# A two-layer mLSTM and pooling block: input sums stored in HBM and read back behind the last value tile, and a 128-byte filler

## The chip, the cores and the metric

The kernel runs on one core of a Trainium2 chip. The metric is the device time of one execution in microseconds (us). The engines are named as the profile names them: PE is TensorE (PEld its weight loads), DVE is VectorE, ACT is ScalarE, POOL is GpSimd and SP issues the DMAs.

## The reference

The model has two layers on 1024 latent tokens (model width 1024, inner width 2048) with 256 context tokens. Layer 0 is a bidirectional mLSTM mixer. Its input `h`, the normed and modulated tokens, is multiplied by three weight blocks:

```
xm, z, og = split(h @ w_in, 3)          # each 2048 wide
xc = silu(short_conv(xm)); q, k = headwise(xc); v = headwise(xm)
gates = [q, k, v] @ w_gate              # input and forget gates, both directions
y = (sigmoid(og) * norm(mlstm(q, k, v, gates)) + skip * xc) * silu(z);  out = y @ w_out
```

Layer 1 is a pooling mixer on the 16 x 64 token grid. The change touches layer 0 only: the forming of operands for the `z` and `og` products, and one address.

## The kernel before, in words

Every product is made from three fp32r matmuls: an fp32 operand `x` is split into a rounded part `hi` and a rest `lo`, and `hi*hi + hi*lo + lo*hi` is summed in PSUM (`mm3`, lines 142 to 145). So the layer's input lies in SBUF as pairs of tiles, `h[k, hf]` for the eight blocks k of 128 channels and the two halves hf of 512 tokens.

The work is staged as follows.

1. **Features** (lines 339 to 376, loop 491 to 500). For n = 0 to 15, PE forms 128 columns of `xm` for all tokens, and ACT and DVE form the convolution. The loop lies in a hand-written PE order. Between its matmuls stand those of `token_part(n - 1)` (lines 378 to 410): ten small products give the values of the previous tile, and DVE reduces each of them into a tile `vst` (line 397). The value tile of n = 15, the last, is left over, and is done between the first ten steps of the next stage.
2. **Block sums** (lines 503 to 519). For k = 0 to 3, POOL adds hi and lo of `h[k]` and `h[k+4]` back to fp32 into two tiles `t0`, `t1` (line 508). DVE forms four differences and sums of their halves (lines 512 to 515), ACT rounds each (518), and DVE takes the rest (519). The result is `T_[1..4, k]`, the right-hand operands of four products of a Strassen scheme.
3. **Plain products** (`plain`, lines 591 to 607). The first pair of `z` tiles and the first pair of `og` tiles are formed without Strassen. `count` numbers their 64 steps, each of three matmuls of 512 columns. Steps 1 to 10 pull the last value tile along. At steps 12, 15, 27 and 50 (`GATE_STEPS`) a piece of `gates()` (lines 416 to 487) follows: copies of the gate sums; transposes (423) and a chain of small DVE operations (424 to 450); transposes (457) and the running scans (466 to 470) with what follows them (474 to 477); and the last transposes (482, 486).
4. **Strassen products** (`strassen`, lines 526 to 567) for the 14 remaining pairs: seven products of four blocks in place of eight. In order they are a11 with plain `h`, s2 with `T_[2]`, s3 with `T_[3]`, a12 with plain `h`, s1 with `T_[1]`, a22 with `T_[4]`, and s4 with plain `h`. POOL forms s1 to s4 from the weights (lines 535 to 538).
5. **Scores and values** of 4 heads x 8 token tiles (lines 703 to 797, about 675 to 1270 us). In `values` (773), 30 matmuls per step have as weights the decayed scores, transposed into the tiles `pt` (`turn`, 757 to 766), and move value tiles `S4`.
6. The output product of layer 0, layer 1, and the output.

**Buffers.** Tiles are drawn by tag. The tag `T5` has five buffers in this part (the profile writes `T`), and the features' tiles `xp`, `y` and `vst`, the sums' `t0` and `t1`, the gates' tiles (`g32`, `lft`, `it_`, `lf_r`, `i_r`, `b_r`, `m_r`) and the Strassen tiles `r2`, `s12` and `s34` all draw from it. A tile waits until an earlier tile of its tag has had its last use. `S4` (profile: `S`) has 32 buffers of 4096 bytes, `wh`, `wl` and `wr` two of 4096 each, `pt` six of 2048. One pool holds them in the order in which they are first named: `S4`, `wh`, `wr`, `wl`, then `cst` (1152 bytes), `mask` (512), `amat` (256), then `pt`, then `hn` (three of 2048) and smaller tiles; the `T5` pool lies behind.

**Order.** Except for the hand-written stretches of PE, a scheduler that simulates the engines' times sets the order of each engine's instructions when the program is built. On the chip each engine takes its instructions in that order, and SP issues the DMAs in that order too.

## Time and profile before

| | us |
|---|---|
| median of 3 runs (2099.69 to 2103.97) | 2099.81 |
| the profiled execution, its own time | 2102.29 |
| its span, first to last instruction | 2100.6 |

PE is busy for 95% of the span, DVE for 64%, ACT for 37% and POOL for 23%. Busy time of PE includes matmuls that run at half clock, so a busy PE is not always a fast one. All times of day below are us from the start of the span.

### The profile page before, as it was taken

To read this page: it belongs to the slowest core of one execution; us is meant where nothing else is said; L and a number is where in the kernel's file an instruction comes from. 1 tells how busy PE (TensorE), PEld (TensorE's weight loads), DVE (VectorE), ACT (ScalarE), POOL (GpSimd) and SP (SyncE) were. 2 spreads that over 40 slices of the span, in tenths; PEclk is the share of its full clock that TensorE was granted. 3 is DMA by queue.
4 is the path that set the end of the run, shared out by engine and by line. 5 is a ranking of instruction groups with operands and counts; after the bars stand their busy time and mean duration, and the time that the engine had idled before them with its cause. 6 is when DMAs were issued, how large, how long until landed. Compare 5 with 4: busy or idle time off the path is not lost.

```text
span 2100.6 us, 26372 instructions
## 1 busy us (share of the span) xinstructions
PE 1994.7 (95%) x10050; PEld 1673.2 (80%) x10050; DVE 1335.8 (64%) x2136; ACT 773.3 (37%) x1201; POOL 486.5 (23%) x482
## 2 busy tenths in 40 slices
PE   7899996799999899999999999999999999999997
PEld 5688885688888787787878787888788888888897
DVE  4877777976777868667676663353567273754444
ACT  5444443333333533433324332443433132223443
POOL 4400003233222313331332311161200000000275
PEclk9999998899999999999999999999999999999999
DMA  7133332154443635245234143434331222124473
GB/s 295 73 113 108 104 107 88 49 163 146 141 131 121 230 126 154 77 147 164 81 110 151 41 157 129 171 131 140 120 121 56 78 73 71 60 96 158 157 263 126
DMA packets 156032, 263.94 MB, mean 126 GB/s; under 512 B 10077, under 2 KB 89437, under 8 KB 155905
## 3 DMA queue, kind: packets, MB, share of 16 engines
q1 hardware_dynamic: 155904, 262.25, 37.5%
q8 instruction: 79, 1.29, 0.2%
q14 instruction: 49, 0.39, 0.1%
HBM read 201.21 MB, written 61.00 MB: 125 GB/s over the span
## 4 chain that ended last, share of the span: by engine, by line
PE 66%; DVE 9%; POOL 3%; DMA 3%; issue 3%; ACT 1%; SPq 0%; DVEq 0%; POOLq 0%; ACTq 0%
PE pa L131 30%; PE pc L131 29%; PE pb L131 5%; PE pb L762 1%; DMA wr<-in_w_ada_dram 1%; POOL hn L931 1%; POOL S L951 1%; DVE wl L631 1%; DVE T L753 1%; DVE T L721 1%; DVE T L755 1%; DVE den L749 1%; PE pc L793 1%; DVE T L754 0%; DVE S L863 0%
## 5 line engine op out<-in xcount | busy, mean ns | idle before, releaser
L131 PE MATMUL pa<-S,wh 128*128 128x512 f32 (+1 forms) x2496 | 721.4, 373 | 8.3 <-DVE S L303 8.2
L131 PEld LDWEIGHTS pa<-S,wh 128*128 128x128 f32 x2496 | 444.7, 190 | 80.9 <-DVE S L303 11.9
L131 PE MATMUL pa<-S,wl 128*128 128x512 f32 (+1 forms) x1248 | 460.1, 369 | 0.4 <-DVE wl L139 0.3
L131 PE MATMUL pc<-S,wh 128*128 128x512 f32 (+1 forms) x1616 | 452.6, 366 | 2.8 <-ACT wh L137 1.9
L131 PEld LDWEIGHTS pc<-S,wh 128*128 128x128 f32 x1616 | 293.0, 189 | 53.0 <-ACT wh L137 2.1
L139 DVE TENSOR_TENSOR wl<-wr,wh 128x1024 fp32r<-128x1024 f32 (+1 forms) x124 | 146.8, 1184 | 272.3 <-ACT wh L137 271.3
L131 PE MATMUL pc<-S,wl 128*128 128x512 f32 (+1 forms) x808 | 294.1, 366 | 1.2 <-DVE wl L139 1.0
L137 ACT ACTIVATE wh<-wr 128x1024 fp32r<-128x1024 f32 (+1 forms) x124 | 124.6, 1005 | 404.8 <-PE pa L131 177.7
L131 PEld LDWEIGHTS pa<-S,wl 128*128 128x128 f32 x1248 | 236.0, 189 | 40.8 <-DVE wl L139 1.0
L131 PE MATMUL pa<-S,S 128*128 128x512 f32 (+1 forms) x1152 | 253.1, 369 | 14.5 <-DVE T L721 14.5
L131 PE MATMUL pc<-S,pt 128*128 128x512 f32 x960 | 237.6, 401 | 0.0
L131 PEld LDWEIGHTS pa<-S,S 128*128 128x128 f32 x1152 | 196.3, 194 | 46.8 <-issue 11.5
L131 PEld LDWEIGHTS pc<-S,pt 128*128 128x128 f32 x960 | 180.1, 191 | 39.5
L131 PEld LDWEIGHTS pc<-S,wl 128*128 128x128 f32 x808 | 152.6, 189 | 26.4 <-DVE wl L139 1.8
L931 POOL TENSOR_TENSOR hn<-hn,pt 128x512 f32<-128x512 f32 (+1 forms) x48 | 80.6, 1681 | 298.6 <-ACT pt L930 288.2
L764 ACT ACTIVATE pt<-pb 128x512 fp32r<-128x512 f32 (+1 forms) x96 | 48.7, 522 | 180.8 <-PE pb L762 138.6
L397 DVE TENSOR_REDUCE T<-pb 128x144 f32<-128x288 f32 x160 | 72.3, 454 | 59.6 <-PE pb L131 59.3
L721 DVE SCALAR_TENSOR_TENSOR T<-pa,T 128x256 f32<-128x256 f32 (+3 forms) x184 | 76.6, 454 | 36.9 <-PE pa L131 31.1
L642 POOL TENSOR_TENSOR S<-S,S 128x1024 fp32r<-128x1024 f32 x35 | 89.2, 2567 | 41.7 <-ACT S L641 41.7
L765 DVE TENSOR_TENSOR pt<-pb,pt 128x512 fp32r<-128x512 f32 (+1 forms) x96 | 56.5, 597 | 37.2 <-ACT pt L764 36.7
L545 ACT ACTIVATE wh<-T 128x512 fp32r<-128x512 f32 x70 | 42.5, 626 | 99.2 <-POOL T L538 55.6
L131 PE MATMUL pb<-S,wh 128*128 128x512 f32 x256 | 78.9, 389 | 0.0
(322 smaller groups left out, 2529.6 us busy)
## 6 DMA issues: line engine op xcount, KB each, us to landing
wr<-in_bw_in_dram SPq DMA_DIRECT2D x40, 512.0 KB, 3.5
wr<-in_w_in_dram SPq DMA_DIRECT2D x34, 512.0 KB, 3.8
S<-xc_d SPq DMA_DIRECT2D x34, 512.0 KB, 5.2
wr<-in_w_ada_dram SPq DMA_DIRECT2D x32, 512.0 KB, 3.7
wr<-in_w_out_dram SPq DMA_DIRECT2D x32, 512.0 KB, 3.5
T<-in_bw_out_dram SPq DMA_DIRECT2D x32, 512.0 KB, 4.4
S<-y_d SPq DMA_DIRECT2D x28, 512.0 KB, 7.0
v_d<-T SPq DMA_DIRECT2D x16, 640.0 KB, 3.9
```

The costliest lines, as they stand in the source:

```text
L131: PE.matmul(out, lhsT, rhs, start=start, stop=stop)
L137: S.activation(h, r, AF.Copy)
L139: V.tensor_tensor(l, r, f(h), op=ALU.subtract)
L397: V.tensor_reduce(vst[:, s], p.rearrange("p a b -> p b a"), axis=AX.X, op=ALU.add)
L545: S.activation(hi, a, AF.Copy)
L631: V.scalar_tensor_tensor(a, w, csil[:, k, 0:1], a, op0=ALU.mult, op1=ALU.add)
L642: eng.tensor_tensor(t, f(t), f(u), op=ALU.subtract)
L721: V.scalar_tensor_tensor(W[:, lo + sh:hi + sh], p[:, lo - o:hi - o], 1.0, W[:, lo + sh:hi + sh], op0=ALU.mult, op1=ALU.mult, accum_out=dp[ ...
L749: V.tensor_tensor(r, r, emt[:, ti, h:h + 33:32], op=ALU.max)
L764: S.activation(th[:, :n], p[:, :n], AF.Copy)
L765: V.tensor_tensor(tl_[:, :n], p[:, :n], f(th[:, :n]), op=ALU.subtract)
L931: G.tensor_tensor(acc, acc, sq, op=ALU.add)
```

## The change

Each of POOL's additions is done earlier, one k per feature tile n = 2 to 9, into an `S4` tile, and the fp32 sum is stored in HBM (`h_d`). The block sums become a function `sums(k)` that is called at steps 16, 24, 32 and 40 of the plain products. It loads `t0` and `t1` from `h_d` in place of having POOL add them; the DVE and ACT operations are the same as before. A tile `pad1` of 128 bytes per partition, which nothing uses, is named between `amat` and the first `pt` tile.

```diff
+SUM_STEPS = (16, 24, 32, 40)
...
+    h_d = dr.tile([KD, P, T], F32, name="h_d")
...
     amat = const([P, KE, 4], "amat")
+    const([P, 32], "pad1")
...
             if n == 2:
                 bilinear()
+            if 2 <= n < 2 + KD:
+                hs = tl("S4", [P, T])
+                for hf in range(2):
+                    G.tensor_tensor(hs[:, hf * 512:hf * 512 + 512], f(h[n - 2, hf][0]), f(h[n - 2, hf][1]), op=ALU.add)
+                nc.sync.dma_start(h_d[n - 2], hs)
             parts.append(token_part(n, *out))
...
         T_ = {}
-        for k in range(4):
+
+        def sums(k):
             t0, t1 = tl("T5", [P, T]), tl("T5", [P, T])
             for t, kk in ((t0, k), (t1, k + 4)):
-                for hf in range(2):
-                    G.tensor_tensor(t[:, hf * 512:hf * 512 + 512], f(h[kk, hf][0]), f(h[kk, hf][1]), op=ALU.add)
+                nc.sync.dma_start(t, h_d[kk])
             b11, b12, b21, b22 = t0[:, :512], t0[:, 512:], t1[:, :512], t1[:, 512:]
...
                         if count in GATE_STEPS:
                             next(steps, None)
+                        if count in SUM_STEPS:
+                            sums(SUM_STEPS.index(count))
```

## Rows read from the trace of the kernel before

**Rows 1.** The page, its head and busy times.

```profile
span 2100.6 us, 26372 instructions
PE 1994.7 (95%) x10050; PEld 1673.2 (80%) x10050; DVE 1335.8 (64%) x2136; ACT 773.3 (37%) x1201; POOL 486.5 (23%) x482
```

**Rows 2.** What PE waited for: in total, times, longest.

```profile
PE pb L131 <- DVE T L397: 27.7, 1, 27.7
```

**Rows 3.** Busy time by stretch; the clock is after POOL's count.

```profile
core 0: us, PE busy (x) PEld busy (x) DVE busy (x) ACT busy (x) POOL busy (x), PEclk, DMA share, GB/s
330.00:346.00 16.00, 16.00 (x92) 13.79 (x92) 10.71 (x19) 6.08 (x9) 5.09 (x4) 1.00 0.29 94
...
349.70:377.50 27.80, 0.07 (x1) 0.00 (x0) 27.49 (x25) 7.51 (x12) 20.34 (x12) 0.56 0.09 37
377.50:383.00 5.50, 5.50 (x16) 4.37 (x17) 5.50 (x11) 3.19 (x5) 0.63 (x1) 0.50 0.01 1
383.00:391.20 8.20, 8.20 (x42) 6.40 (x41) 7.83 (x17) 2.90 (x5) 0.14 (x1) 0.97 0.18 53
391.20:434.70 43.50, 41.36 (x207) 33.41 (x207) 34.15 (x47) 14.30 (x23) 12.75 (x7) 1.00 0.34 107
```

**Rows 4.** DVE in order of time around the stall: start, duration, line, operands.

```profile
352.21 1.76 DVE L512 TENSOR_TENSOR T<-T,T 128x512 f32<-128x512 f32 x1
...
371.26 0.68 DVE L512 TENSOR_TENSOR T<-T,T 128x512 f32<-128x512 f32 x1
...
375.33 1.75 DVE L514 TENSOR_TENSOR T<-T,T 128x512 f32<-128x512 f32 x1
377.00 0.81 DVE L397 TENSOR_REDUCE T<-pb 128x144 f32<-128x288 f32 x2
...
379.91 1.88 DVE L519 TENSOR_TENSOR S<-T,S 128x512 fp32r<-128x512 f32 x3
```

**Rows 5.** POOL in order of time; in brackets its idle time and what ended it.

```profile
334.35 2.55 POOL L508 TENSOR_TENSOR T<-S,S 128x512 f32<-128x512 f32 x2 [17.38 <-DVE T L365]
...
373.22 3.31 POOL L508 TENSOR_TENSOR T<-S,S 128x512 f32<-128x512 f32 x2 [3.04 <-DVE S L519]
...
414.99 2.60 POOL L535 TENSOR_TENSOR T<-T 128x512 f32<-128x512 f32 x1 [23.30 <-DVE T L470]
417.66 2.16 POOL L536 TENSOR_TENSOR T<-T,wr 128x512 f32<-128x512 f32 x1
```

**Rows 6.** PE in order of time, gate transposes and the second Strassen product.

```profile
391.19 0.80 PE L423 MATMUL pb<-ident,T 32*128 32x32 f32 x10
...
401.95 0.40 PE L457 MATMUL pb<-ident,T 128*36 128x128 f32 x2 [0.38 <-ACT T L458]
...
434.52 0.62 PE L131 MATMUL pc<-S,wh 128*128 128x512 f32 x2
```

**Rows 7.** DVE in order of time, scans and what follows them.

```profile
402.80 0.68 DVE L466 TENSOR_TENSOR_SCAN hn<-T,zero 36x256 f32<-36x256 f32 x1 [2.40 <-ACT T L458]
403.51 2.34 DVE L467 TENSOR_TENSOR_SCAN T<-T,hn,zero 36x1024 f32<-36x1024 f32 x1
...
412.51 2.34 DVE L470 TENSOR_TENSOR_SCAN T<-T,hn,T 4x1024 f32<-4x1024 f32 x1
...
418.70 2.20 DVE L477 TENSOR_TENSOR T<-T,T 36x1024 f32<-36x1024 f32 x1
420.83 0.73 DVE L577 SCALAR_TENSOR_TENSOR hn<-hn,vec,pt 128x512 f32<-128x512 f32 x1
```

**Rows 8.** DMA issues from 340 to 440 us: KB each, median us to landing.

```profile
v_d<-T SPq DMA_DIRECT2D x2, 640.0 KB, 4.1
T<-in_w_in_dram SPq DMA_DIRECT2D x2, 512.0 KB, 3.7
```

**Rows 9.** Line 508, POOL's additions: duration in ns, minimum, median and maximum.

```profile
L508 POOL TENSOR_TENSOR T<-S,S x16: 1287/1674/2513, 334.3 to 374.8; 128x512 f32<-128x512 f32 x16
```

**Rows 10.** The chain that ended last: start, duration, matmuls of one run.

```profile
434.68 2.72 PE pc L131 x12
...
761.80 6.97 PE pc L131 x30
...
782.13 2.73 PE pa L131 x12
```

## The prediction

> **What bounds the kernel now.** I read the page first: PE is busy for 1994.7 of 2100.6 us [rows 1], so only the 106 us in which PE idles, stretches at half clock, and the matmuls' own pace can be won. The view of PE's waits comes next; its longest single wait is 27.7 us, on one DVE reduction of a value tile [rows 2]. The table of stretches places it: PE does nothing from 349.7 to 377.5, DVE is full (27.49 of 27.80) and POOL nearly so. [...]

> The timeline of DVE says why. From 352.2 DVE forms block sums; the first reduction for the last value tile (line 397) starts at 377.00, just after the work on the second k [rows 4]. In the code the four pairs `t0`, `t1` are named before the last `vst`, and they share five T5 buffers. The reader is to see that the reduction has no buffer until a block sum gives one back. POOL bears out that buffers go in the order of naming: it could add at any time, but began at 334.35, when line 365 of the feature tile gave a buffer up, and later additions begin when line 519 has [rows 5].

> **The change, part by part.** The sum is made against the profiled execution, 2102.29 us; it stands 2.5 above the median of 2099.81, and I carry the difference over to that median.

> *The stall goes.* The last `vst` is now named before any `t0`, so PE walks on at 349.7. Up to the gate transposes (line 423, at 391.19 [rows 6]) it has 5.5 us of work at half clock, 2.75 at full, and 8.2 us at nearly full [rows 3], together 11.0. These transposes come at 360.7; I take 361.0, since ten reductions and the convolution keep DVE nearly full there. So far 30 us are won: 27.7 of idle, 2.75 of clock.

> *How much is kept depends on the second Strassen product* (s2 with `T_[2]`), which starts at 434.52 [rows 6] and needs line 519's results of all four k. PE could be there at 404.0 (434.5 - 27.7 - 2.75). In the new order of naming the T5 buffers go: `vst`, `g32`, `lft`, `it_`, `lf_r`, `i_r`, two pairs of `t`, `b_r`, `m_r`, two more pairs, `r2`, `s12`, `s34`. Five buffers make this a ring, which I follow step by step.
> - The last 457 transposes of `lft` end at 402.35 [rows 6], 11.2 us after line 423; now at 372.2. Only then has the second tile of pair 0 a buffer. A load of the same size lands after 3.7 us [rows 8]: 375.9.
> - One k is four sums and four rests on DVE. Three rests took 1.88 us [rows 4], so 0.63 each and 5.0 per k, undisturbed. Pair 0 is free at 380.9, its first tile near 380.3.
> - That buffer goes to pair 1 (load to 384.0), the other to `b_r`. Now scans of `b` run as well: two of 0.68 and two of 2.34 [rows 7], 6.0. Pair 1's 5.0, these 6.0 and, as an estimate, 3.4 of gating work and weight rests end at 395.3. Pair 1, earlier in the program, is through near 390.5 and gives `m_r` and one tile of pair 2 their buffers.
> - The scans of `m` (6.0) and one gating step (1.5, two of 0.73 [rows 7]) end at 402.5. `lf_r` is free, and pair 2 can be loaded: 406.2.
> - Lines 474 to 477, the store of `i_r` (bounded by 4.1, the larger store of [rows 8]) and the transposes of `b_r` free two buffers by 407: pair 3 is there at 410.7, `r2` at about 410.
> - Pair 2 is through at 411.2. In pair 3 the needed rest lies 3.1 us further, 414.3. But POOL forms s1 and s2 then, and beside POOL a DVE sum took 1.76 in place of 0.68 [rows 4], POOL's own steps 2.60 and 2.16 [rows 5]. That moves both operands to about 417.

> So s2 starts near 417 in place of 434.5: 17.5 us. PE runs out of other work before: it could start s2 at 404, and a12, ahead of its turn, takes 2.72 [rows 10], to 407. Ten idle us follow, and they cost the clock once more, some 2.7 as before, and the product done early gives 2.7 back. For work of DVE that is still behind (two gating steps) I add 1. Stage: -16.5. The bounds are -30.5 (PE never waits) and, with every DVE step beside POOL, a loss (rival 2).

> *Sixteen additions and eight stores move to feature tiles 2 to 9, eight loads to the plain products.* POOL idled 17.38 us there before its first addition [rows 5], so 2 x 1.67 us per tile [rows 9] fit. DVE steps beside them lengthen by some 1.1 each, and PE waits on DVE's reductions. But in 330 to 346 POOL already made four additions beside a feature tile, and PE was busy 16.00 of 16.00 [rows 3]. I take 0 and bound it at 8 x 0.5 = 4 for a later reduction per tile. Below 0 nothing is in reach, with PE full. On SP each store waits for POOL's sum, and each load for its buffer; behind them are weight loads, which have half a tile's time to spare, and the gating step's loads and stores, which PE does not read. One `S4` buffer is held for a POOL sum and a store of about 4 us; by the code the features hold 20 of 32 for the input and four for each of two tiles, so it finds a place.

> *The filler.* In the values, 30 matmuls with `pt` weights take 6.97 us, 232 ns each; 12 with other weights take 2.72, 227 each [rows 10]. By the code's sizes, 1152 + 512 + 256 = 1920 bytes lie between `wl` and `pt`, so `pt` is 128 bytes off from `S4` and `wh` modulo 256; with the filler it stands as they do. If that is the reason for the 5.7 ns, a step saves 0.17 us, and 32 steps 5.5. Some of it falls beside DVE work that PE waits for, so I take -4.5. The bounds are -5.5, and +5.5 if the T5 and `hn` tiles, which move too, lose as much.

> [...]

> **Sum:** -16.5 - 4.5 = -21.0, on the median 2078.8: 2079.

> **The rivals.**
> 1. *The loads are in time* and PE never waits: -30.5 - 4.5 = -35.0, 2065. For it: DVE has 34.15 busy of 43.5 in this stretch [rows 3], with room for some of the 20 us of sums. Against it: the ring. Chance 0.24.
> 2. *Slower.* Each round of the ring is a load and eight DVE steps. If these run beside POOL, or behind a scan in DVE's fixed order, a round is 3.7 + 8 x 1.7 = 17.3 us. From 372.2, four rounds and 12 of scans end at 453, 19 later than today: 2119 without a gain of the filler. It decides from rounds of 12.6 on, (434.5 - 372.2 - 12) / 4; my forecast has 8.2 on average. POOL has nothing else to do in that stretch, which speaks against it. Chance 0.06.
> 3. *Rounds near 12*, so that the stall only changes its name: within 4 us of 2099.8. Chance 0.04.
> 4. *The filler changes nothing*, the ring as forecast: 2083.5. For it: the rows give a pace and not its reason. Against it: runs of 12 with other weights in the same part, such as the one at 782, keep 227 [rows 10]. Chance 0.21.

> **How the numbers follow.** My forecast, ring and filler both, has 0.45. A measurement tells 0.2% here, 4.2 us, from no change. Forecast, 1 and 4 lie beyond that on the fast side: 0.90. Rival 3, and the 0.01 of rival 2 with rounds barely over 12.6, stay within it: 0.05. The rest of rival 2 is slower: 0.05. The range reaches from rival 1 (2065, less 1) to a ring 8 us later than I have it, without the filler: 2083.5 + 8 = 2092.

> **What would show it.** Right: PE's wait on line 397 falls under 3 us and the clock stays full from 350 to 400; a new wait of PE of about 10 us stands before the product with `T_[2]`, ended by DVE's rests, with a stretch at 0.50 behind it; the sums' loads are issued when `lft`, then pair 0, then `lf_r` are done; the feature stretch keeps PE full; 30 matmuls with `pt` weights take 6.80. Wrong in the ring: no wait at s2 (rival 1), or one that ends past 434 (rival 2). Wrong in the filler: 6.97 again. A loss of PE in 110 to 240 us would refute the zero for the additions.

## The result, and the profile after

| | before | after |
|---|---|---|
| median of the runs, us | 2099.89 (4 runs, 2099.69 to 2103.97) | 2086.68 (4 runs, 2084.41 to 2087.14) |
| ratio, 95% interval | | 0.993 (0.9913 to 0.9948) |
| the profiled execution, us | 2102.29 | 2086.98 |
| its span, us | 2100.6 | 2085.2 |

The change makes the kernel 13.2 us faster, 15.3 between the two profiled executions. The forecast was 21; 2079 lies 7.7 below the median, and the range (2064 to 2092) holds it. In the changed kernel line 131 is 133, 397 is 400, 423 is 426, 450 is 453, 457 is 460, 466 to 470 are 469 to 473, 512 to 515 are 520 to 523, 519 is 527 and 545/546 are 553/554; line 516 has the sums' loads.

What PE waits for, in the changed kernel (in total, times, longest), from the view that [rows 2] came from:

```profile
PE pc L133 <- ACT wh L553: 6.3, 1, 6.3
...
PE pb L460 <- DVE T L453: 3.7, 1, 3.7
...
PE pc L133 <- DVE wl L554: 2.9, 1, 2.9
```

The wait of 27.7 us [rows 2] has no row any more. Three smaller ones stand behind it: at the transposes of the gate tiles, at the second Strassen product's weights, and at the rests of these weights.

The same part by stretches (busy time of the engines, granted clock after POOL's count), beside [rows 3]:

```profile
374.50:384.00 9.50, 7.75 (x28) 5.11 (x29) 8.38 (x11) 4.97 (x10) 0.00 (x0) 0.51 0.20 69
384.00:411.60 27.60, 27.60 (x132) 22.40 (x131) 22.53 (x27) 7.15 (x11) 0.00 (x0) 1.00 0.52 154
411.60:422.00 10.40, 1.28 (x3) 0.50 (x2) 10.33 (x11) 6.71 (x11) 6.53 (x4) 0.64 0.28 64
422.00:428.60 6.60, 6.54 (x16) 5.15 (x17) 3.48 (x7) 1.15 (x2) 2.65 (x2) 0.53 0.86 262
```

PE now loses time twice: 374.5 to 384.0 goes at 0.51 of the full clock, and between 411.6 and 422.0 it works for 1.28 of 10.40 us, with a stretch at 0.53 behind it. DVE is full in that second hole (10.33 of 10.40). PE in order of time (start, duration, in brackets the idle time and what ended it):

```profile
374.53 2.30 PE L460 MATMUL pb<-ident,T 128*36 128x128 f32 x10 [3.71 <-DVE T L453]
...
417.96 1.22 PE L133 MATMUL pc<-S,wh 128*128 128x512 f32 x2 [6.30 <-ACT wh L553]
...
422.06 0.80 PE L133 MATMUL pc<-S,wl 128*128 128x512 f32 x1 [2.88 <-DVE wl L554]
```

**Where the 15 us come from.** Both kernels issue 10050 matmuls on PE, so the start of the same one, counted along PE, can be compared. I took the differences (after less before) at eight of them and subtract each from the next; times are those of before. Below, this table is called the ledger. It compares one traced execution of each version.

| from, to | what runs there | us |
|---|---|---|
| start, 106 | loads, first products | -0.12 |
| 106, 141 | feature tiles, first part | +0.56 |
| 141, 344 | feature tiles, the others | +0.45 |
| 344, 450 | last value tile, gates, plain and first Strassen products: *the stage* | -10.78 |
| 450, 723 | Strassen products | +0.05 |
| 723, 1295 | the values, with `pt` weights | -4.39 |
| 1295, 1613 | the passage to the next layer | -1.48 |
| 1613, 2083 | the rest, up to the 10000th matmul | +1.21 |

The sum is -14.5, and the tail behind it gives 0.9 more: the span's 15.4. The experiments below are read with this table.

The values' gain shows in the chain that ended last: 30 matmuls with `pt` weights took 6.97 us before [rows 10] and take 6.84 after.

```profile
751.73 6.84 PE pc L133 x30
```

### The profile page after: what moved, and what is told of

Same layout as the page of the kernel before. It is cut to its first block, busy times and chain, and to the rows that moved or that the text cites. A ratio compares the mean times of both kernels' runs of the same rounds, so it can differ in the third digit from the quotient of the medians.

```text
span 2085.2 us, 26407 instructions
## 1 busy us (share of the span) xinstructions
PE 1994.8 (96%) x10050; PEld 1674.5 (80%) x10050; DVE 1329.5 (64%) x2136; ACT 772.6 (37%) x1201; POOL 475.4 (23%) x482
## 4 chain that ended last, share of the span: by engine, by line
PE 79%; DVE 12%; DMA 3%; issue 3%; POOL 2%; ACT 1%; SPq 0%; DVEq 0%; POOLq 0%; ACTq 0%
PE pa L133 40%; PE pc L133 31%; PE pb L133 6%; PE pb L772 1%; POOL S L961 1%; DMA wr<-in_w_ada_dram 1%; DVE S L306 1%; DVE wl L641 1%; DVE T L763 1%; DVE T L731 1%; POOL hn L941 1%; DVE T L765 1%; DVE S L304 1%; DVE den L759 1%; PE pc L803 1%
## 5 line engine op out<-in xcount | busy, mean ns | idle before, releaser
L133 PE MATMUL pa<-S,S 128*128 128x512 f32 (+1 forms) x1152 | 251.1, 367 | 14.6 <-DVE T L731 14.6
L133 PEld LDWEIGHTS pa<-S,S 128*128 128x128 f32 x1152 | 195.7, 194 | 46.0 <-issue 11.6
```

The costliest lines, as they stand in the source:

```text
L133: PE.matmul(out, lhsT, rhs, start=start, stop=stop)
```

## The experiments

Each version was profiled once and timed 4 to 12 times, against the kernel before on the same chip. The versions are spread over several chips, and the executions of one version spread by 1.3 to 11.5 us, so across chips the ratios compare better than the medians. In the table, *features* is the step from 106 to 344 us and *stage* that from 344 to 450, both against before as above.

| version | median us | ratio (95%) | features | stage |
|---|---|---|---|---|
| the changed kernel | 2086.68 | 0.9930 (0.9913-0.9948) | +1.0 | -10.8 |
| without the filler | 2088.67 | 0.9938 (0.9926-0.9949) | +0.4 | -12.5 |
| filler of 256 bytes | 2090.41 | 0.9945 (0.9931-0.9958) | +0.4 | -12.5 |
| before, with the filler alone | 2099.61 | 0.9989 (0.9979-0.9999) | +0.6 | -0.1 |
| POOL adds at the new place | 2093.73 | 0.9964 (0.9951-0.9977) | +0.6 | -5.3 |
| stored copy, sums first | 2093.66 | 0.9965 (0.9952-0.9977) | +1.0 | -7.6 |
| gates at 12, 24, 46, 62 | 2090.40 | 0.9941 (0.9928-0.9955) | +1.0 | -11.6 |
| gates last | 2085.95 | 0.9926 (0.9915-0.9938) | +1.0 | -14.3 |
| differences on POOL too | 2083.43 | 0.9910 (0.9894-0.9925) | +4.2 | -23.2 |
| that, one gate buffer, later gates | 2077.56 | 0.9881 (0.9866-0.9896) | +4.3 | -23.4 |
| one gate buffer, later gates, DVE's differences | 2082.15 | 0.9906 (0.9890-0.9923) | +1.0 | -18.8 |
| the last but one, POOL's steps spread | 2077.07 | 0.9879 (0.9864-0.9893) | +3.7 | -24.1 |
| that, last gating step in the Strassen group | 2080.90 | 0.9903 (0.9884-0.9921) | +3.7 | -24.3 |

### Without the filler

```diff
-    const([P, 32], "pad1")
```

> The changed kernel without the tile pad1; everything else as changed. Theory (place: pt weights that lie 128 bytes off the moving tiles, modulo 256, are slower): 30 matmuls with pt weights take 6.97 us again in place of 6.80, and the time is 4 to 5 us above the changed kernel's 2086.7, about 2091. Rival (the pace came from what other engines do in that part, or from the order of the rest): the 30 matmuls keep 6.80 and the time stays within 1 us of 2086.7.

The time rose to 2088.67 us, by 2.0 and not by the 4 to 5 that I expected; but the values lost what they had gained: the step from 723 to 1295 is -0.35 in place of -4.39. In the chain that ended last the runs of 30 are back at the pace of before:

```profile
752.35 6.96 PE pc L133 x30
```

The features show the reverse: +0.43 in the first tiles, and 0.00 from 141 to 344 us, where the changed kernel loses 0.45. So the additions on POOL cost 0.4 us in all, and the filler the rest. The stage is 1.7 us shorter than the changed kernel's; the values' 4.0 less 0.6 and 1.7 make 1.7, which fits the 2.0 between the medians. The intervals of the two ratios overlap, so the reading rests on the pace and the ledger, not on the medians.

### A filler of 256 bytes

```diff
-    const([P, 32], "pad1")
+    const([P, 64], "pad1")
```

> The changed kernel with a filler of 256 bytes in place of 128. Theory (place modulo 256 against the moving tiles): the pt tiles stand 128 bytes off again, so 30 matmuls take 6.97 us and the time is about 2091, as without a filler. Rival (any move of the tiles is enough, or the old addresses were bad for a reason of their own): 6.80 and 2086.7.

Everything behind the filler moves here too, but the pace is that of before:

```profile
751.62 7.00 PE pc L133 x30
```

The values give -0.85, the features +0.42 and 0.00, the stage -12.45: within half a us the kernel without a filler. So it is not enough that something was moved: 128 bytes further is fast (6.84 us), 0 and 256 are slow (6.96 and 7.00), as the theory had it for these three; no other distance was tried. The filler moves `pt` and every tile named behind it; that it is `pt` follows from the matmuls that change pace, which read `pt` and the unmoved `S4` tiles alone, and was not tried by itself.

### The kernel before, with the filler alone

```diff
     amat = const([P, KE, 4], "amat")
+    const([P, 32], "pad1")
```

> The kernel before with the tile pad1 added and nothing else. Theory: the 27.7 us wait on the last value tile stays, 30 matmuls with pt weights take 6.80 us, and the time is 4 to 5 us below 2099.9, about 2095.5. Rival (the filler pays only together with the moved sums): within 1 us of 2099.9.

The values give -4.53 and the pace is the changed kernel's:

```profile
764.06 6.84 PE pc L131 x30
```

The features lose 0.11 and 0.45 without any addition in them, the same 0.45 as in the changed kernel. The stage is untouched (-0.13), the stall of 27.7 us included. The time missed my 2095.5: the median is only 1.9 us under the one measured beside it (2101.47), with an interval from 0.2 to 4.4 us. Of the 4.5, 0.6 go in the features, and the runs on that chip spread over several us (2095.4 to 2106.9).

### POOL adds at the new place

The changed kernel without the stored copy.

```diff
-            if 2 <= n < 2 + KD:
-                hs = tl("S4", [P, T])
...
-                nc.sync.dma_start(t, h_d[kk])
+                for hf in range(2):
+                    G.tensor_tensor(t[:, hf * 512:hf * 512 + 512], f(h[kk, hf][0]), f(h[kk, hf][1]), op=ALU.add)
```

> The changed kernel with its new order and its filler, but without the stored copy: POOL adds into t0 and t1 at the four new places, as it did before the change. It tells the new place apart from the copy. Theory: the place alone removes the stall of 27.7 us on the last value tile, and the copy only shortens each round of the T5 buffers. Then PE's wait on line 397's reduction stays away, and the 0.9 us lost in the features come back; but a pair costs POOL 4 additions of 1.67 us, 6.7 in all instead of a load of 3.7, and DVE's eight steps run beside POOL at up to 1.76 us. The wait before the second Strassen product grows from 6.3 us to between 12 and 25, and the time is 2095, from 2091 to 2103. Rival: the copy removed the stall, and without it a wait of over 15 us stands again before 360 us, with 2096 to 2104. A second rival: the rounds are hidden, and the time stays within 2 us of the changed kernel's 2086.7.

The place alone removes the stall: no wait on the last value tile is left. The other two waits grow (numbering of this version, 459 for 460 and 548 for 553):

```profile
PE pb L459 <- DVE T L452: 8.8, 1, 8.8
PE pc L132 <- ACT wh L548: 7.9, 1, 7.9
```

The time, 2093.73, is near the 2095 expected, though most of the loss went to the gates (8.8 in place of 3.7) and not, as I had it, to the second product. The stage keeps 5.3 of its 10.8 us. So the move is what ends the stall, and the copy is worth 5.5 us of what follows it.

### The stored copy, with the sums first

```diff
-SUM_STEPS = (16, 24, 32, 40)
+SUM_STEPS = ()
...
+        for k in range(4):
+            sums(k)
         steps = gates()
         count = 0
```

> The changed kernel with its stored copy and its filler, but all four pairs of sums named ahead of the plain products, where the kernel before had them. It tells the copy apart from the place. Theory: the stall came from the place, because the last value tile gets its T5 buffer only after the pairs named before it, whoever forms the additions. DVE's four sums and four rests of a k take 5.0 us at least, so the four pairs take 20 from about 350, less what the first pairs do ahead of it: a wait of 10 to 20 us on line 397's reduction (line 400 in its numbering) before 375, half a clock's cost of about 2.7 behind it, and then no wait before the second Strassen product. The time is 2084, from 2078 to 2090, about that of the changed kernel by another way. Rival: POOL's additions were the reason, and a load in their place removes the stall at the old place too: the wait is under 4 us, nothing waits later, and the time is 2066, from 2063 to 2071.

The stall is back, 19.9 us at line 400, with loads and without one addition on POOL in this part:

```profile
PE pb L133 <- DVE T L400: 19.9, 1, 19.9
```

The rival, that POOL's additions made the stall, is out. The time was missed: 2093.7 against 2084. The stage is 3.2 us worse than the changed kernel's (the wait is at the upper end of what I gave), and 3.0 more go in the passage to the next layer and behind it, which the section on the prediction comes back to.

### Gates at 12, 24, 46 and 62

```diff
-GATE_STEPS = (12, 15, 27, 50)
-SUM_STEPS = (16, 24, 32, 40)
+GATE_STEPS = (12, 24, 46, 62)
+SUM_STEPS = (12, 14, 18, 22)
```

> The changed kernel with SUM_STEPS (12, 14, 18, 22) and GATE_STEPS (12, 24, 46, 62): the block sums come ahead of the gates' scans, so the four pairs get T5 buffers before the gates' tiles and the gate chain on DVE is not in a hurry. Theory (what is left of the stall is order: a gate chain cut up by sums, then r2's buffer that hangs on the scans): PE's wait on the gate transposes of 3.7 us with its half clock, and the 9 us before the second Strassen product, go for the most part; that product starts 10 to 16 us earlier, at 404 to 410, and the time is 2071 to 2078. Rival (DVE has too much to do in this stretch whatever the order: 68.5 us busy of 81.7): the wait turns up in another place and the time stays at 2084 to 2089.

The wait before the second Strassen product is gone, and two others have its length:

```profile
PE pb L460 <- DVE T L453: 9.6, 1, 9.6
...
PE pb L485 <- DVE T L480: 5.6, 1, 5.6
```

All sums are formed by 394 us here, and the gating chain is through only at 394.9: DVE is busy for 28.64 of the 29.90 us from 365 to 394.9, and then idles for 2.96 us (the next version's text has it full up to 397, which it is not). The stage is -11.6, little better than the changed kernel's: the wait moved. The time, 2090.40, is over the rival's 2084 to 2089 too. The traced execution is the slowest of the six; beside the changed kernel's, its ledger loses 1.7 us before 106, 2.4 in the values and 3.2 behind them.

### Gates last

```diff
-GATE_STEPS = (12, 15, 27, 50)
-SUM_STEPS = (16, 24, 32, 40)
+GATE_STEPS = (12, 24, 62)
+SUM_STEPS = (12, 14, 18, 22)
...
             prod([w_in[KE + n + i] for i in range(2)], lambda i, hf, t: z_done(n, sz, i, hf, t))
+            if n == 2:
+                next(steps, None)
```

> The changed kernel with the sums named at the plain products' steps 12, 14, 18 and 22, the gates' transposes at 24, the transposes of the row tiles with the scans at 62, and the gates' last step behind the first Strassen product group. It moves each gating step that PE takes part in away from the 20 us in which DVE forms the sums. Theory: PE waited on DVE's order, 3.7 us at the gating transposes and 9.2 before the second Strassen product, and half a clock each time; with the sums ahead of the gates all four k are formed by 396, the gates' chain has 20 us before PE needs it, and PE runs from 350 to 404 without a wait over 2 us. The time is 2073, from 2069 to 2079. Rival: DVE itself is full in this stretch (it was in the version with gates at 12, 24, 46 and 62, from 365 to 397), so that any order only moves the wait: one or two waits of 5 to 10 us stand again between 395 and 430, and the time is 2084 to 2091.

The gates now cost PE 2.1 us, and the second product 12.8:

```profile
PE pc L133 <- ACT wh L553: 12.8, 1, 12.8
...
PE pb L460 <- DVE T L453: 2.1, 1, 2.1
```

The rival's time came (2085.95 in 2084 to 2091). Why the wait is there can be read on POOL (idle time and what ended it in brackets):

```profile
415.79 1.44 POOL L543 TENSOR_TENSOR T<-T 128x512 f32<-128x512 f32 x1 [26.60 <-DVE T L473]
```

Line 543 forms s1, and its T5 buffer comes free with the last scan (line 473). The scans, put off to step 62, hold the buffers that the Strassen sums need. So both of my theories had half: DVE's order sets where the wait is, and the five buffers tie the scans to the sums. The stage is 3.5 us better than the changed kernel's.

### The differences on POOL too

POOL forms the four sums and differences of a k beside feature tiles 2, 4, 6 and 8 and stores both tiles; DVE's lines 520 to 523 go.

```diff
+            if n in (2, 4, 6, 8):
...
+                G.tensor_tensor(b22, b22, b12, op=ALU.subtract)
+                G.tensor_tensor(b12, b12, b11, op=ALU.subtract)
+                G.tensor_tensor(b11, b22, b11, op=ALU.add)
+                G.tensor_tensor(b21, b21, b11, op=ALU.subtract)
...
-            V.tensor_tensor(b22, b22, b12, op=ALU.subtract)
...
```

> The changed kernel, but POOL forms the four sums and differences of each k beside the feature tiles too, and both tiles are stored ready; after the loads DVE has only the four rests of a k. It takes 16 DVE steps of 0.69 us, 11 us, out of the stretch, and changes no order. Theory: DVE's sums between the steps of the gates and of the ring are what PE waits on, so the gates' chain ends 3 to 4 us after its transposes as before the change (9 us instead of 12), the wait of 3.7 falls under 1 with the half clock behind it, and each of the four rounds of the buffers is 2 us shorter, which brings the second Strassen product 4 to 8 us forward. The time is 2079, from 2075 to 2083. Rival: the second product hangs on the load of r2 and the scans alone, and the gates' chain on other work; then less than 3 us are won, 2084 to 2087. A third way: POOL's 32 more steps beside the feature tiles slow DVE there and PE waits; up to 5 us are lost before 344.

The wait before the second product is down to 0.3 us; the one at the gates stayed:

```profile
PE pb L460 <- DVE T L453: 3.9, 1, 3.9
```

So the stage gained 12.4 us more than the changed kernel, the largest step of all. I had expected the second product 4 to 8 us earlier; it begins 4.3 earlier, at 413.70, though the features lost 3.2 more. The time, 2083.43, lies just over the range that I gave, 2075 to 2083. The third way held as well: the features lose 4.2 us in place of 1.0. From 110 to 240 us PE is busy for 127.71 us (130.00 before, 129.88 in the changed kernel), with POOL at 45.56 in place of 21.02. The changed kernel first, this version below it:

```profile
110.00:240.00 130.00, 129.88 (x735) 110.94 (x733) 93.72 (x179) 54.18 (x79) 21.02 (x38) 1.00 0.40 134
...
110.00:240.00 130.00, 127.71 (x709) 107.28 (x708) 100.71 (x176) 53.00 (x77) 45.56 (x57) 1.00 0.40 130
```

### One buffer for both gate tiles, and later gates, with POOL's differences

```diff
-GATE_STEPS = (12, 15, 27, 50)
-SUM_STEPS = (16, 24, 32, 40)
+GATE_STEPS = (12, 15, 38, 62)
+SUM_STEPS = (16, 18, 20, 22)
...
-        lft, it_ = tl("T5", [P, 10, 64]), tl("T5", [P, 10, 64])
+        li = tl("T5", [P, 2, 10, 64])
+        lft, it_ = li[:, 0], li[:, 1]
```

> The version in which POOL forms sums and differences beside the features, with two more edits: the two gate tiles lft and it_ share one T5 buffer, so that two pairs of the sums and the gates need no buffer from each other, and all four pairs are named at steps 16 to 22, with the transposes of the gate tiles at 38 and the gates' last step at 62. Theory: what the changed kernel lost of its 29.6 us was 7.7 at the gates' transposes and 13.1 before the second Strassen product, both made of DVE's order and of T5 buffers that wait for scans. With 11 us less on DVE, all four pairs through by 390 and the transposes 7 us later, PE has no wait over 1.5 us and no stretch at 0.50 between 360 and 430, and the second product starts at 404 to 407. The features still cost the 4.4 us that they did in the version with POOL's differences. The time is 2074, from 2070 to 2079. Rival: DVE is full here too, and one wait of 5 us or more, with half a clock, stands somewhere between 380 and 420: 2080 to 2086.

The time, 2077.56, lies in the theory's range, but not for its reason. The wait at the gates is still there, as the rival had it, with the granted clock at 0.80 from 375 to 392 us:

```profile
PE pb L461 <- DVE T L454: 4.1, 1, 4.1
```

The stage is -23.4, the same as without these edits. The 5.9 us between the two medians come from later parts, where the two programs do the same work: by the ledger 2.9 us are won before 723, 3.6 in the passage to the next layer and 1.1 behind it, and 1.5 are lost in the values. The first of these is the clock, and the border at 723 cuts through its effect: taken together with the values it is 1.4. At the entry to the values PE waits in either version, and the 38 matmuls behind take 7.63 us in this one:

```profile
694.02 7.63 PE L133 MATMUL pa<-S,S 128*128 128x512 f32 x38 [3.54 <-DVE T L736]
```

In the version before:

```profile
694.59 10.18 PE L133 MATMUL pa<-S,S 128*128 128x512 f32 x38 [3.48 <-DVE T L735]
```

From 680 to 700 us the granted clock is 1.00 here and 0.83 there.

### The same two edits, DVE's differences kept

The last diff, on the changed kernel.

> The changed kernel, its differences still on DVE, with the other two edits of the same kind: lft and it_ in one T5 buffer, the four pairs named at steps 16 to 22, the transposes of the gate tiles at 38 and the last gating step at 62. It tells the buffers and the order apart from DVE's amount of work. Theory: DVE has 20 us of sums, some 8 of gating steps and 12 of scans between 361 and 404, 40 of 43 us beside the weight rests, so the buffers alone don't suffice: a wait of 3 to 8 us stays at the transposes or before the second product, and the time is 2081, from 2077 to 2087. Rival: the buffers were all that was missing, and it runs as fast as it would with the differences on POOL, less the 4.4 us that these cost in the features: 2067 to 2073.

2082.15, within the 2077 to 2087 expected, with its longest wait, 5.1 us, at the gates:

```profile
PE pb L461 <- DVE T L454: 5.1, 1, 5.1
```

There is none before the second product, which begins at 416.50. From 380 to 392 us DVE is busy for 11.63 of 12.00, and PE for 6.18 at 0.51 of the clock; from 392 to 410 DVE has 17.71 of 18.00:

```profile
380.00:392.00 12.00, 6.18 (x24) 3.79 (x25) 11.63 (x23) 7.06 (x14) 0.00 (x0) 0.51 0.23 88
392.00:410.00 18.00, 17.03 (x77) 13.74 (x76) 17.71 (x14) 3.42 (x6) 3.54 (x2) 0.95 0.33 98
```

With this order and one buffer fewer in use the stage gains 8.0 us over the changed kernel, and DVE is then full. Which of the two edits does it was not tried. POOL's differences bring the stage 4.6 further and cost the features 3.3.

### POOL's steps spread over twelve tiles

```diff
-            if n in (2, 4, 6, 8):
+            if 2 <= n < 14:
+                k, r = divmod(n - 2, 3)
...
```

> As the version with POOL's differences, one buffer for the gate tiles and the later steps, but POOL's 32 steps are spread over feature tiles 2 to 13, two or three per tile, in place of eight in each second tile. It tests where the features' 4.4 us come from. Theory: PE waits where POOL's steps come in a clump and lengthen the DVE steps of one tile by more than the tile has to spare; spread, a tile has at most 4 us of them, as in the changed kernel (3.3 per tile, 0.9 us lost in all). The features then lose 0.5 to 2 us, and the time is 2071, from 2067 to 2076. Rival: each POOL step costs the same wherever it stands, and the features lose 4 to 5 us again: within 1.5 us of the version without the spread.

2077.07 beside 2077.56 on the same chip, 1.2% under before; the executions of either spread over nearly 4 us, so the two are level. The theory missed: the features lose 3.7 us, not 0.5 to 2; the spread saves 0.6. Nearer to the truth is the rival, that a POOL step costs about the same wherever it stands. PE waits on line 400's reductions, 1.22 us in the first of these tiles:

```profile
114.23 0.47 PE L133 MATMUL pb<-vv,S 128*128 128x288 f32 x2 [1.22 <-DVE T L400]
```

### The last gating step inside the Strassen group

```diff
-GATE_STEPS = (12, 15, 38, 62)
-SUM_STEPS = (16, 18, 20, 22)
+GATE_STEPS = (12, 13, 46)
+SUM_STEPS = (18, 20, 22, 24)
...
+                if n == 2 and (i, hf) == (0, 0):
+                    next(steps, None)
```

> As the version with POOL's steps spread, with the steps of the gates moved again: the gates' transposes at step 13, the four pairs at 18 to 24, the transposes of the gate tiles at 46 in place of 38, and the gates' last step inside the first Strassen group, after its first finished block. In the version before, PE waited 4.2 us at the transposes at step 38 and 1.2 at the last step, with about 2 of half clock behind the first. Theory: PE arrives at 46 at 386.4, when the gating chain is through (385.5), so both waits and the half clock go, 7 us; POOL can form s1 and s2 only when the last scan gives their buffer back, near 403, so that a wait of 2 to 4 us stands before the second Strassen product. The time is 2073, from 2070 to 2076. Rival: the scans now end later, as much as the transposes are moved, and the wait before the second product is over 6 us with the clock falling again: within 1.5 us of the 2077 of the version before, or over it.

Both waits at the gates are gone, and 4.9 us stand before the second product:

```profile
PE pc L133 <- ACT wh L562: 4.9, 1, 4.9
```

The stage is -24.3 beside -24.1: the wait moved again, though it is shorter than the 6 us that the rival asked for. POOL and DVE in order of time say what made it long:

```profile
403.62 1.38 POOL L552 TENSOR_TENSOR T<-T 128x512 f32<-128x512 f32 x1 [48.64 <-DMA ga_d<-hn]
405.08 4.58 POOL L553 TENSOR_TENSOR T<-T,wr 128x512 f32<-128x512 f32 x1
```

```profile
403.77 2.31 DVE L478 TENSOR_TENSOR T<-T,T 36x1024 f32<-36x1024 f32 x1
406.01 0.74 DVE L594 SCALAR_TENSOR_TENSOR hn<-hn,vec,pt 128x512 f32<-128x512 f32 x1
406.67 1.21 DVE L481 TENSOR_TENSOR T<-T,T 36x1024 f32<-36x1024 f32 x1
407.80 0.74 DVE L600 SCALAR_TENSOR_TENSOR hn<-hn,vec,pt 128x512 f32<-128x512 f32 x1
```

The step that forms s2 took 4.58 us while DVE ran its lines 478, 594, 481 and 600, where it took 1.71 in the changed kernel. The time missed the 2070 to 2076 and is 3.8 us over the version before, on another chip (about 5 by the ratios). Between the two traced executions, 5.4 us apart, the ledger has 3.6 in the passage to the next layer and 1.6 behind it, tail included; ahead of the passage they differ by 0.2.

## Why the prediction was right, and where it was not

The median missed the forecast by 7.7 us. Of these, 5.7 are the stage (-10.8 for -16.5), 1.0 is the features, and 2.1 come from the traced execution before, which stood further above its median than the one after; the passage to the next layer, which I did not have, gives 1.5 back, and the rest is 0.4.

**The stall, right.** Line 426's transposes start at 361.63, forecast 361.0; that is 29.6 us earlier than before [rows 6], or 30.5 without what the features lost. The place is the reason: it brings the stall back with the copy kept (19.9 us), and its change removes it with POOL still adding. That it acts by the T5 buffers, as I had it, and not by DVE's fixed order alone fits the rows, but was not tried apart.

**The ring, right in its end and wrong on the way.** I let the buffers go in the order in which the tiles are named. The rows fit another rule: they go to the tile whose first writer comes first in the order of the scheduled program. Pair 0 was loaded from 357.58 and 362.47, not at 372.2 when `lft` is done, and half of pair 1 at once behind it (start, duration, line and number of issues on SP's queue):

```profile
357.58 0.32 SPq L516 DMA_DIRECT2D T<-h_d  x1
...
362.47 1.02 SPq L516 DMA_DIRECT2D T<-h_d  x2
...
399.43 0.32 SPq L516 DMA_DIRECT2D T<-h_d  x1
...
404.51 0.91 SPq L516 DMA_DIRECT2D T<-h_d  x1
405.51 0.38 SPq L539 DMA_DIRECT2D T<-in_w_in_dram  x1
```

The later pairs hung on the scans and on their forerunners as forecast: pair 3's second tile was asked for at 404.51 and `r2` at 405.51, and DVE began on pair 3 at 410.63 (forecast 410.7), POOL on s1 at 412.31 (forecast 410 for `r2`). The second Strassen product began at 417.96, forecast 417. That it is so near is in part luck: the scans ended at 392.6 in place of some 401, pair 3's last load was asked for 2.5 us before its time (404.5 for 407.0), and it took 6.0 us in place of 3.7. What released it was POOL's s2 (line 544, 415.53 to 417.24) and ACT's cast of it; `T_[2]`'s last rest, the one I named, was out at 416.1.

**What failed: the price behind that start.** My term was: the idle time costs the clock once more, 2.7; "the product done early gives 2.7 back"; and 1 us for DVE work still behind; from -17.5 to -16.5. The runs show -16.6 at the start of the product (434.52 to 417.96) and -9.9 at 450 us. Of the 6.7 lost, 3.6 lie before 422.06: two matmuls that took 1.22 us where the same two took 0.62 before [rows 6], and 2.88 us until the rest of s2's weights (line 554) came, which stood in DVE's fixed order behind rests that took 1.70 us each beside POOL:

```profile
414.37 5.10 DVE L527 TENSOR_TENSOR S<-T,S 128x512 fp32r<-128x512 f32 x3
...
421.32 1.28 DVE L554 TENSOR_TENSOR wl<-T,wh 128x512 fp32r<-128x512 f32 x2
```

The other 3.0 are the clock of 0.53 from 422.0 to 428.6 (6.6 x 0.47 = 3.1). Nothing was given back: PE's order has the products as the code names them, and a12 did not run ahead. The term should have been 6.7 in place of 1.0, and the stage -10.8 in place of -16.5. I had priced a weight rest "as an estimate" among 3.4 us of DVE work, but not as the second operand for which PE stands still.

**A wait that I did not have.** At the gates' transposes PE waited 3.71 us, and ran at 0.51 of the clock up to 384.0; by the same-matmul count that took 7.7 us (-29.6 to -21.9). The chain from line 427 to 453 runs from 362.48 to 374.14, with pair 0's four sums and four rests between its steps, from 366.08 to 372.9: 5.3 us of the 11.7. I had sized DVE for the ring and not for this chain. The clock did not stay full from 350 to 400, which I had named as a sign of being right. By my reading the wait cost little in the end, since PE without it would have waited longer for the same product at 417.96; moving the gates later gave 0.8 (12, 24, 46, 62) and 3.5 (last) in the stage.

**The additions, nearly right.** Forecast 0, bound 4; measured 0.4 by the two versions with additions and without the shift. That the whole features lost 1.0 and not 0.4 is the filler's doing (0.6 with the filler alone). With 32 POOL steps in place of 16, and 45.56 us of POOL in place of 21.02 between 110 and 240 us, the loss is 4.2: the cover that I named, PE full and 17.38 us of idle POOL [rows 5], carries the sixteen additions and not much more.

**The filler, right in the values and smaller on the time.** Forecast -4.5; the values gave -4.39 with the change and -4.53 without it, 30 matmuls took 6.84 us (forecast 6.80), and 6.96 to 7.00 where `pt` was not moved by 128 bytes. In the chains that ended last, all runs of 30 with `pt` weights take 6.81 to 6.92 us in the eleven profiles with the shift, and 6.96 to 7.08 in the three others. My upper bound named other tiles that may lose by the move: the features did, 0.6 us. In the changed kernel the stage, too, is 1.7 us longer with the filler than without; with the filler alone it is not, and why is open. So on the whole time the filler was worth 2.0 and 1.9 us by the two pairs of medians, and not 4.5.

**The rivals.** The first (PE never waits) fell by the waits of 6.3 and 2.9 us. The second and third asked for rounds of 12 us and more; the product came at 417.96, far before 434.5. The fourth fell with the pace, and by the pace alone: the median lies nearer to its 2083.5 than to 2079.

Two slips of the prediction moved nothing: POOL was busy for 20.34 of 27.80 us in the stall [rows 3], which is not nearly full, and 395.3 with 6.0 and 1.5 makes 402.8, not 402.5.

**Not foreseen.** The passage to the next layer (1295 to 1613 us) gave -1.48. It has two forms in these runs. In one, PE waits 0.3 us in all on POOL's `hn` there (the changed kernel, the three on the filler, POOL's additions at the new place, one gate buffer with either engine's differences, the spread); in the other 4.0 (before, the sums first, both moved gates, POOL's differences, the last version), and this part is 1.5 to 3.6 us longer. It follows none of the edits, and every engine has the same operations on the same tiles in the same order there in all fourteen profiles. The traces show what differs: seven POOL steps that form `hn` begin 2.5 us behind seven DVE steps in each of them, and one engine goes ahead at the other's cost. The changed kernel, then the version with POOL's differences:

```profile
1452.70 6.50 DVE L961 TENSOR_TENSOR S<-S,S 128x512 f32<-128x512 f32 x7
1455.20 12.63 POOL L941 TENSOR_TENSOR hn<-hn,pt 128x512 f32<-128x512 f32 x7 [10.22 <-ACT pt L940]
1461.46 0.50 PE L133 MATMUL pa<-S,wl 128*128 128x512 f32 x1 [3.32 <-DVE wl L141]
...
1444.59 4.30 DVE L965 TENSOR_TENSOR S<-S,S 128x512 f32<-128x512 f32 x7
1447.09 14.57 POOL L945 TENSOR_TENSOR hn<-hn,pt 128x512 f32<-128x512 f32 x7 [10.22 <-ACT pt L944]
1461.72 1.87 PE L133 MATMUL pb<-ones,hn 128*128 128x1 f32 x8 [3.64 <-POOL hn L945]
```

All eight profiles of the first form have 6.5 and 12.6 to 12.7 us, all six of the second 4.3 and 14.6. PE then waits for a rest of weights or for `hn`, and the clock makes the rest of the difference: 0.66 from 1461.5 to 1466.5 in the changed kernel, 0.50 from 1462 to 1467 with POOL's differences, 1.00 from 1450 to 1460 with the spread. What decides which engine goes ahead is open, and so is whether a version keeps its form from one execution to the next. Part of what the medians of the versions differ by is this and not the stage: of the 3.5 us that the last gates win in the stage most are lost so, and 3.6 us of the difference between the two versions with POOL's differences come from it.

**What beats both.** Eleven us of DVE steps moved to POOL, one buffer for both gate tiles and POOL's steps spread: 2077.07 us, ratio 0.9879. Of the 30.5 us that the stall was worth, the stage then keeps 24.1, less 3.7 in the features.

## What to carry to other kernels

When a stall ends, price the next chain up to the last operand that PE needs, every operand of it (a weight's high part, its rest, the moving tile) and the slower clock behind it (0.53 for 6.6 us here): in this kernel these were 6.7 us behind a start that was forecast to 1 us. Where an engine's order is fixed and the buffers form a ring, a wait that is taken away by shifting steps tends to come back elsewhere (9.6 and 5.6, 12.8, 4.9 us in three orders); what shortened the stage was less work on the full engine (12.4 us), or one buffer fewer in use together with a new order (8.0). Compare the same instruction along the bounding engine in two traces before believing a difference of the medians: it showed that more than half of the features' loss was the filler's and that a gain of 5.9 us was not where its edit was. One trace is one execution, though: the same steps in the same order shared out in two ways here, 1.5 to 3.6 us apart.
